# The order of two heads' small products on TensorE: one head after the other, or alternating

## The chip, the cores and the metric

The kernel runs on one core of a Trainium2 chip. The metric is the time of one execution in device microseconds, as the median of several runs.

## What is computed

One layer of a hybrid decoder for 256 prompt tokens and 8 sample tokens (T = 264 columns; activations stand transposed, features on the partitions):

```
x = x + 0.5 * swiglu(rmsnorm(x, n1), f1g, f1u, f1d)
proj = rmsnorm(x, nm) @ w_in                    # 2048 -> 4864
o_att  = sink_attention(q, k, v)                # 16 heads of 64, window 128, blocks of 128
o_rwkv = rwkv_time_mix(proj[..., ATT_COLS:])    # 16 heads of 64, matrix state 64 x 64
x = x + concat(o_att, o_rwkv) @ w_out
x = x + 0.5 * swiglu(rmsnorm(x, n2), f2g, f2u, f2d)
```

The recurrence of one time-mixing head, per token, which the kernel computes for the prompt in four chunks of 64 tokens:

```
sa = S @ (-kk);  S = S * exp(logw) + outer(sa, kk * a) + outer(v, k);  y = S @ r
```

## The kernel before

**The large products.** Both feed-forward parts, the projections (`win`) and the output product (`wout`) go through `gemm`: a chunk of up to 512 weight columns is loaded (`raw`, SP queue), ScalarE casts it to `hi` (line 121), VectorE takes the rest `lo` (line 56), and TensorE does three products per 128 x 128 block with 264 columns. Their results (`acc`) have three banks. Every product goes through the helper `mm`, so most of TensorE's rows carry line 72.

**The mixing stage** (`mixing_body`). The 16 time-mixing heads stand as eight pairs: head 0 of a pair has partitions 0 to 63, head 1 partitions 64 to 127 (`HALF`). The pairs form four batches of two (`BATCH`). Each piece of work is a generator that stops at `yield`; every chunk of a large product calls `tick`, which lets each generator go one step further. The order of calls is `SEQ`: the projections of the four batches, then of keys and values, then of the eight query tiles; then the output product in three passes (`PASS`), ahead of which the tasks that it needs are drained. A scheduler then puts the instructions of each engine in order; each engine works through its own list in that order. Small products (`m`) share five banks (`NM`), taken in turn with `mp()`.

Of the generators, these hold the lines that the change touches:

- `prep` (lines 356 to 458), once per pair: decay and keys, then **Gram blocks** (lines 420 to 433): for each head four products of `BK` (128 columns of one half of the partitions) with `KR` (128 columns) into a bank of the head's own, a masked copy `gm` by VectorE, a transfer of its diagonal blocks to DRAM, and a `yield`. Then two transposes (line 436), the **intermediate keys** `gv` (lines 441 to 446, `gm` with `UV`, 64 x 64 each, both heads in one bank in different partitions), and the transposes of `BK` (lines 447 to 451), which alternate between the heads and use two banks.
- `chain` (lines 470 to 619), once per batch: the diagonal blocks come back (`X`, `Xt`), VectorE solves 30 steps of substitution (`st`, `Xt`), the inverse blocks go out and come back (`TT`). `TN` is their transpose. Then the **corners of the inverse**: 32 x 32 products `gm` with `TN` (lines 515 to 521), copies `zs` (line 525), products `zs` with `TT` (lines 527 to 531), copies into `TT` (line 534). Then **inverse times keys** (`TT` with `KR`, lines 541 to 545) into one bank per pair, copies `W` and `uv`; the **transitions and receptances** (`W` with `BT`, `W` with `gm`, lines 553 to 559), 64 x 64 each, both heads in one bank; products `pN`, `pY`; and three steps over the chunks, whose products with `PT` and `KR` alternate between the heads.
- `attend` (lines 713 to 752), once per query tile, which holds two heads: the two **attention scores** of a head (queries 128 to 255 against 256 keys, queries 0 to 127 against 128 keys, contraction 64) into a bank of its own, the sum with the bias and the maximum (VectorE, line 728), `softmax` (lines 702 to 711), a `yield`; after both heads the transposes of the probabilities (lines 737 to 739) and the products with the values.
- `dec_rwkv` (lines 635 to 667): the state update of the sample tokens, 16 rounds of VectorE and GpSimd work. It and all of batches 0 to 2 are drained ahead of the first pass of the output product, with the attention tasks going on beside them.

In the trace a product stands as out<-moving,weights; a 32-bit product appears as two instructions. `kr,bk` is a Gram block, `uv,gm` with 64 x 64 the intermediate keys, `TN,gm` and `TT,zs` the corners, `kr,TT` inverse times keys, `t,W` and `gm,W` transitions and receptances, `s,q` scores, `C,t` of lines 737 to 739 the transposes of the probabilities.

Of the kernel before, what the change touches and what calls it, by code (L numbers as in the profile page):

```python
# [10 lines left out]
ALU = mybir.AluOpType  # L11
AX = mybir.AxisListType

P = 128
NP = 256
# [9 lines left out]
HALF = (slice(0, 64), slice(64, 128))  # L25
# [20 lines left out]
def body(tc, I, O):  # L46
    nc = tc.nc
    V, A, G, TE, SP = nc.vector, nc.scalar, nc.gpsimd, nc.tensor, nc.sync
# [6 lines left out]
    def tt(e, out, a, b, op):  # L55
        return e.tensor_tensor(out=out, in0=a, in1=b, op=op)  # L56
# [11 lines left out]
    def bc(ap, shape):  # L68
        return ap.broadcast_to(list(shape))

    def mm(out, lhsT, rhs, start=True, stop=True, **k):
        TE.matmul(out, lhsT, rhs, start=start, stop=stop, **k)  # L72
# [20 lines left out]
    with ExitStack() as ctx:  # L93
# [17 lines left out]
        def mp():  # L111
            return pp.tile([P, 512], F32, tag="m", bufs=NM, name=uid("m"))
# [176 lines left out]
        def mixing_body(mx, n2, n3):  # L289
# [12 lines left out]
            tri, msk = C[:, CTR:CTR + P], C[:, CMK:CMK + P]  # L302
# [53 lines left out]
            def prep(p, bt, k, xrr, xk, xv):  # L356
# [39 lines left out]
                BK, KR = ring((P, 4, 3, 64), "bk", 2), ring((P, 3, 4, 64), "kr", NKR)  # L396
# [20 lines left out]
                tt(V, bv, bps[:, :T], xv, ALU.mult)  # L417
                G.tensor_copy(bvdec[:, p, :], bv[:, NP:T])
                yield
                for h in range(2):  # L420
                    r = HALF[h]
                    gp = mp()
                    for c in range(4):
                        mm(gp[:, c * P:(c + 1) * P], BK[r, c, h:h + 2, :], KR[r, 0:2, c, :])
                    gm = ring((P, 4, P), "gm", NGM)
                    bt.Gm[k][h] = gm
                    tt(V, gm, gp.rearrange("p (c t) -> p c t", c=4), bc(msk.unsqueeze(1), (P, 4, P)), ALU.mult)
                    for blk in range(2):
                        x = blk * 32
                        SP.dma_start(  # L430
                            scr[bt.i].rearrange("(h b k c) (s t) -> h b k s c t", h=2, b=2, c=4, s=32)[h, blk, k],
                            gm[h * 64 + x:h * 64 + x + 32, :, x:x + 32])
                    yield
# [5 lines left out]
                        A.copy(KR[HALF[h], 0, e:4:2, :],  # L439
                               kp[HALF[e], :256].rearrange("p (c t) -> p c t", c=2)[:, :, HALF[h]])  # L440
                gv = mp()
                for h in range(2):
                    r, o = HALF[h], HALF[1 - h]
                    for c in range(4):
                        mm(gv[r, c * 64:c * 64 + 64], bt.Gm[k][h][o, c, 0:64], bt.UV[o, c, k, r])
                A.copy(KR[:, 2], gv[:, :256].rearrange("p (c t) -> p c t", c=4))
                bps = [mp(), mp()]
                for c in range(4):
                    for h in range(2):
                        r = HALF[h]  # L450
                        mm(bps[h][:, c * 64:c * 64 + 64], BK[r, c, h:h + 2, :], ident[r, r])
                for tb in range(2):
                    t = tmp((P, 2, P))
# [16 lines left out]
            def chain(bt):  # L470
                n = bt.n
# [17 lines left out]
                for s in range(1, 31):  # L489
                    m, w = -(-s // ng), 31 - s  # L490
                    t = ring((ng * nr, m, w), "st", 2)
# [8 lines left out]
                for h in range(2):  # L500
                    for blk in range(2):
                        x = h * 64 + blk * 32
# [3 lines left out]
                for h in range(2):  # L506
                    for blk in range(2):
                        x = h * 64 + blk * 32
# [4 lines left out]
                    V.transpose(TN[h * 64:h * 64 + 32], TT[h * 64:h * 64 + 32, :, 0:32])  # L513
                yield
                ps = mp()
                for h in range(2):
                    for k in range(n):
                        for c in range(4):
                            j = k * 4 + c
                            mm(ps[h * 64 + 32:h * 64 + 64, j * 32:j * 32 + 32],  # L520
                               bt.Gm[k][h][h * 64:h * 64 + 32, c, 32:64], TN[h * 64:h * 64 + 32, j, :])
                zs = ring((P, n * 4, 32), "zs", 1)
                for h in range(2):
                    r = slice(h * 64 + 32, h * 64 + 64)
                    A.copy(zs[r], ps[r, :n * P].rearrange("p (c t) -> p c t", t=32))
                yield
                ps = mp()
                for h in range(2):
                    r = slice(h * 64 + 32, h * 64 + 64)
                    for j in range(4 * n):  # L530
                        mm(ps[h * 64:h * 64 + 32, j * 32:j * 32 + 32], zs[r, j, :], TT[r, j, 32:64])
                for h in range(2):
                    r = slice(h * 64, h * 64 + 32)
# [5 lines left out]
                N = ring((P, n, 4, 64), "N", 1)  # L539
                wus = [mp() for _ in range(n)]  # L540
                for k in range(n):
                    for h in range(2):
                        r = HALF[h]
                        for c in range(4):
                            mm(wus[k][r, c * P:c * P + P], TT[r, k * 4 + c, :], bt.KR[k][r, 0:3:2, c, :])
                for k in range(n):
                    v = wus[k].rearrange("p (c t) -> p c t", c=4)
# [3 lines left out]
                yield  # L551
                pbs = [mp() for _ in range(n)]
                for k in range(n):
                    for h in range(2):
                        r = HALF[h]
                        for c in range(1, 4):
                            x = (c - 1) * P
                            mm(pbs[k][r, x:x + 64], W[r, k, c - 1, :], bt.BT[k][c // 2][r, c % 2, r])
                            mm(pbs[k][r, x + 64:x + P], W[r, k, c - 1, :], bt.Gm[k][h][r, c, 64:128])
                for k in range(n):  # L560
                    v = pbs[k][:, :384].rearrange("p (c t) -> p c t", c=3)
# [3 lines left out]
                for k in range(n):  # L565
                    for h in range(2):
                        r = HALF[h]
# [3 lines left out]
                for h in range(2):  # L571
                    r = HALF[h]
# [140 lines left out]
            def attend(t, q):  # L713
                p = t // 4
                G.tensor_copy(qd[:, p, :, t % 4], q[:, NP:T])
                bs = [load(I["bias"][(2 * p + h) * 4 + t % 4], (P, 256)) for h in range(2)]
                yield
                sc = []
                for h in range(2):
                    r = HALF[h]  # L720
                    head = (2 * p + h) * 4 + t % 4
                    sps = mp()
                    mm(sps[:, 0:256], q[r, P:NP], kT[p][r, 0:NP])
                    mm(sps[:, 256:384], q[r, 0:P], kT[p][r, 0:P])
                    s1, s0 = tmp((P, 256)), tmp((P, P))
                    mxv = ring((P, 2), "mxv", 6)
                    for s, a, b, j in ((s1, sps[:, 0:256], bs[h], 0), (s0, sps[:, 256:384], bs[h][:, P:256], 1)):
                        V.tensor_tensor_reduce(out=s, in0=a, in1=b, op0=ALU.add, op1=ALU.max, scale=1.0,
                                               scalar=vc(VSK + head), accum_out=mxv[:, j:j + 1])
                    softmax([s1, s0], mxv, vc(VSK + head), 2)  # L730
                    sc.append((s1, s0))
                    yield
                yield from pause(PW[4])
                pt = []
                for s1, s0 in sc:
                    tp = mp()
                    TE.transpose(tp[:, 0:P], s0, ident)  # L737
                    TE.transpose(tp[:, P:2 * P], s1[:, 0:P], ident)
                    TE.transpose(tp[:, 2 * P:3 * P], s1[:, P:256], ident)
                    pa, pb = tmp((P, 256)), tmp((P, P))  # L740
                    A.copy(pa, tp[:, 0:256])
                    V.tensor_copy(pb, tp[:, 256:384])
                    pt.append((pa, pb))
                    yield
                op = mp()
                for h, (pa, pb) in enumerate(pt):
                    r = HALF[h]
                    mm(op[r, 0:256], Vt[p][:, 0, r], pa, True, False)
                    mm(op[r, P:256], Vt[p][:, 1, r], pb, False, True)
                o = slot()  # L750
                A.copy(o[:, :NP], op[:, :NP])
                mixed[8 + t] = o
# [266 lines left out]
```

## Time and profile before

| | |
|---|---|
| Median of 3 runs | 2114.09 us (2106.59 to 2114.15) |
| Profiled execution, its own time | 2113.38 us |
| Span from first to last instruction | 2111.5 us |
| Mean granted TensorE clock | 0.971 |
| Large products into `acc`, instructions | 14736 |
| Transfers | 356.29 MB, mean 169 GB/s |

The profile is that of one execution. Engines are PE (TensorE products), PEld (its weight loads), DVE (VectorE), ACT (ScalarE), POOL (GpSimd) and SP (the queue that issues most transfers). Products are pipelined: the recorded length of one contains its way through the array, so neighbours overlap, and the distance between two starts is the pace. Busy time of a group is the union of its records. A number in brackets with an arrow is idle time ahead of a group and what ended it. The granted clock is the share of full speed that TensorE had.

### The profile page before, as it was taken

The page shows a single profiled execution, that of the slowest core. Times are in us where ns is not written, and L with a number is a line of the kernel's source. Part 1 is how long each engine was busy: PE and PEld are TensorE (multiplying, and loading weights), DVE is VectorE, ACT ScalarE, POOL GpSimd, SP SyncE. Part 2 cuts the span into 40 slices and gives each one's busy share as a digit, 9 for nine tenths or more (in the row PEclk, how much of TensorE's full clock was granted, in tenths as well). Part 3 has the DMA queues.
Part 4 walks back from the last instruction along what each step waited for, and adds up shares of the span by engine and source line. Part 5 has one row for each costly group of instructions (what it writes and reads, how often), then busy time and mean ns, then how long its engine had stood idle before and what let it go on. Part 6 is the DMA issues. An engine that isn't in the chain of part 4 may idle for free.

```text
span 2111.5 us, 45349 instructions
## 1 busy us (share of the span) xinstructions
PE 2045.6 (97%) x16966; PEld 1997.4 (95%) x16966; DVE 1327.7 (63%) x2631; ACT 1061.5 (50%) x2078; POOL 311.1 (15%) x404
## 2 busy tenths in 40 slices
PE   8999999999999999999986899999999999999997
PEld 8999999999999999999975589899999999999997
DVE  5765555556555577876888646756555565655555
ACT  5644444444444576756532444644444444444445
POOL 0301011020101122201044110210110101011012
PEclk9999999999999999999996679999999999999998
DMA  6555565656555574544442155556555565555554
GB/s 221 176 175 187 175 206 170 211 181 181 182 177 185 178 233 150 150 118 129 122 139 79 38 147 183 165 181 181 181 178 184 177 185 182 178 184 175 187 177 139
DMA packets 227535, 356.29 MB, mean 169 GB/s; under 512 B 42177, under 2 KB 83153, under 8 KB 227281
## 3 DMA queue, kind: packets, MB, share of 16 engines
q1 hardware_dynamic: 221616, 344.72, 52.4%
q10 hardware_dynamic: 5696, 8.66, 1.1%
q8 instruction: 133, 2.18, 0.4%
q14 instruction: 90, 0.73, 0.1%
HBM read 345.15 MB, written 10.21 MB: 168 GB/s over the span
## 4 chain that ended last, share of the span: by engine, by line
PE 92%; DVE 4%; DMA 1%; ACT 1%; issue 1%; SPq 0%; DVEq 0%; ACTq 0%
PE acc L72 83%; PE m L72 9%; DVE lo L56 1%; DMA sb<-Xt 0%; DVE ld L56 0%; DMA raw<-in_gu 0%; DVE t L56 0%; DVE st L56 0%; ACT L66 0%; DVE y L56 0%; DVE t L631 0%; DVE s L59 0%; ACT t L66 0%; PE m L737 0%; DVE Xt L56 0%
## 5 line engine op out<-in xcount | busy, mean ns | idle before, releaser
L72 PE MATMUL acc<-s,hi 128*128 128x264 f32 x7072 | 1315.1, 286 | 13.3 <-ACT hi L121 7.7
L56 DVE TENSOR_TENSOR lo<-raw,hi 128x512 fp32r<-128x512 f32 (+2 forms) x1304 | 876.6, 676 | 606.4 <-ACT hi L121 583.2
L121 ACT CAST hi<-raw 128x512 fp32r<-128x512 f32 (+2 forms) x1304 | 780.4, 602 | 879.8 <-PE acc L72 802.2
L72 PEld LDWEIGHTS acc<-s,hi 128*128 128x128 f32 x7072 | 1107.0, 190 | 21.4 <-ACT hi L121 7.7
L72 PE MATMUL acc<-s,lo 128*128 128x264 f32 x3536 | 1013.4, 287 | 2.0 <-DVE lo L56 1.9
L72 PEld LDWEIGHTS acc<-s,lo 128*128 128x128 f32 x3536 | 669.1, 189 | 5.4 <-DVE lo L56 3.9
L72 PE MATMUL acc<-t,hi 128*128 128x264 f32 x2752 | 503.0, 285 | 1.6 <-ACT t L250 1.6
L72 PEld LDWEIGHTS acc<-t,hi 128*128 128x128 f32 x2752 | 426.5, 189 | 1.9 <-ACT t L250 1.8
L72 PE MATMUL acc<-t,lo 128*128 128x264 f32 x1376 | 388.8, 285 | 0.0
L56 POOL TENSOR_TENSOR t<-t,t 128x264 f32<-128x264 f32 (+1 forms) x146 | 156.8, 1074 | 1197.3 <-ACT hi L121 897.5
L72 PEld LDWEIGHTS acc<-t,lo 128*128 128x128 f32 x1376 | 258.4, 188 | 0.0
L56 DVE TENSOR_TENSOR t<-acc,t 128x264 f32<-128x264 f32 x164 | 70.9, 432 | 36.9 <-PE acc L72 36.5
L56 POOL TENSOR_TENSOR s<-s,s 128x264 f32<-128x264 f32 (+1 forms) x56 | 48.7, 871 | 199.0 <-ACT s L66 180.3
L66 ACT ACT_TABLE_LOAD x42 | 53.9, 1283 | 2.9 <-PEq L1011 1.2
L59 DVE SCALAR_TENSOR_TENSOR s<-acc,s 128x264 f32<-128x264 f32 x96 | 40.6, 427 | 16.6 <-PE acc L72 16.1
L59 DVE SCALAR_TENSOR_TENSOR x<-acc,x 128x264 f32<-128x264 f32 x96 | 40.6, 427 | 10.0 <-PE acc L72 9.5
L66 ACT ACTIVATE t<-t 128x264 f32<-128x264 f32 x94 | 40.0, 425 | 3.4 <-DVE t L56 1.9
L250 ACT CAST t<-t 128x264 fp32r<-128x264 f32 x86 | 35.5, 412 | 3.6 <-POOL t L56 2.1
L56 DVE TENSOR_TENSOR st<-X,Xt 128x60 f32<-128x60 f32 (+10 forms) x120 | 28.1, 234 | 12.9 <-DMA Xt<-sa 6.6
L342 POOL COPY shc<-pj 128x9 f32<-128x9 f32 x26 | 20.0, 768 | 85.9 <-DVE pj L56 85.9
L72 PE MATMUL m<-s,hi 128*128 128x264 f32 x160 | 30.3, 289 | 0.3 <-ACT hi L121 0.3
L66 ACT ACTIVATE t<-t,sta 128x256 f32<-128x256 f32 (+2 forms) x33 | 14.7, 446 | 28.3 <-DVE sta L63 27.1
(210 smaller groups left out, 1095.9 us busy)
## 6 DMA issues: line engine op xcount, KB each, us to landing
raw<-in_gu SPq DMA_DIRECT2D x688, 256.0 KB, 3.2
raw<-in_dn SPq DMA_DIRECT2D x224, 256.0 KB, 2.7
raw<-in_win SPq DMA_DIRECT2D x152, 256.0 KB, 3.3
raw<-in_dn SPq DMA_DIRECT2D x160, 192.0 KB, 2.7
raw<-in_wout SPq DMA_DIRECT2D x48, 256.0 KB, 3.0
raw<-in_wout SPq DMA_DIRECT2D x32, 128.0 KB, 2.4
xsp<-x ACTq DMA_DIRECT2D x16, 132.0 KB, 3.5
s<-xsp SPq DMA_DIRECT2D x16, 132.0 KB, 3.0
```

The source lines that it names most:

```text
L56: return e.tensor_tensor(out=out, in0=a, in1=b, op=op)
L59: return V.scalar_tensor_tensor(out=out, in0=a, scalar=s, in1=b, op0=op0, op1=op1)
L66: return A.activation(out=out, in_=in_, func=f, **k)
L72: TE.matmul(out, lhsT, rhs, start=start, stop=stop, **k)
L121: A.copy(hi[:, :w], raw[:, :w])
L250: A.copy(hi, u)
L342: G.tensor_copy(shc[:, t, :], pj[:, NP:NP + NB + 1])
```

## The change

The loops over the two heads of a pair move inside. Gram blocks: both heads take their banks first, and for each chunk head 0's product stands ahead of head 1's; the masked copies, transfers and `yield`s follow per head. Intermediate keys, both corner products, inverse times keys: the loop over heads becomes the innermost. Transitions and receptances: for each chunk both heads' product with `BT`, then both heads' product with `gm`. Scores: both heads take their banks, first the two products with 256 keys, then the two with 128; the softmax follows per head with its `yield`. No product, copy or transfer is added or taken away.

```diff
--- before.py
+++ after.py
@@ -417,14 +417,15 @@
                 tt(V, bv, bps[:, :T], xv, ALU.mult)
                 G.tensor_copy(bvdec[:, p, :], bv[:, NP:T])
                 yield
-                for h in range(2):
-                    r = HALF[h]
-                    gp = mp()
-                    for c in range(4):
-                        mm(gp[:, c * P:(c + 1) * P], BK[r, c, h:h + 2, :], KR[r, 0:2, c, :])
+                gps = [mp(), mp()]
+                for c in range(4):
+                    for h in range(2):
+                        r = HALF[h]
+                        mm(gps[h][:, c * P:(c + 1) * P], BK[r, c, h:h + 2, :], KR[r, 0:2, c, :])
+                for h in range(2):
                     gm = ring((P, 4, P), "gm", NGM)
                     bt.Gm[k][h] = gm
-                    tt(V, gm, gp.rearrange("p (c t) -> p c t", c=4), bc(msk.unsqueeze(1), (P, 4, P)), ALU.mult)
+                    tt(V, gm, gps[h].rearrange("p (c t) -> p c t", c=4), bc(msk.unsqueeze(1), (P, 4, P)), ALU.mult)
                     for blk in range(2):
                         x = blk * 32
                         SP.dma_start(
@@ -439,9 +440,9 @@
                         A.copy(KR[HALF[h], 0, e:4:2, :],
                                kp[HALF[e], :256].rearrange("p (c t) -> p c t", c=2)[:, :, HALF[h]])
                 gv = mp()
-                for h in range(2):
-                    r, o = HALF[h], HALF[1 - h]
-                    for c in range(4):
+                for c in range(4):
+                    for h in range(2):
+                        r, o = HALF[h], HALF[1 - h]
                         mm(gv[r, c * 64:c * 64 + 64], bt.Gm[k][h][o, c, 0:64], bt.UV[o, c, k, r])
                 A.copy(KR[:, 2], gv[:, :256].rearrange("p (c t) -> p c t", c=4))
                 bps = [mp(), mp()]
@@ -513,9 +514,9 @@
                     V.transpose(TN[h * 64:h * 64 + 32], TT[h * 64:h * 64 + 32, :, 0:32])
                 yield
                 ps = mp()
-                for h in range(2):
-                    for k in range(n):
-                        for c in range(4):
+                for k in range(n):
+                    for c in range(4):
+                        for h in range(2):
                             j = k * 4 + c
                             mm(ps[h * 64 + 32:h * 64 + 64, j * 32:j * 32 + 32],
                                bt.Gm[k][h][h * 64:h * 64 + 32, c, 32:64], TN[h * 64:h * 64 + 32, j, :])
@@ -525,9 +526,9 @@
                     A.copy(zs[r], ps[r, :n * P].rearrange("p (c t) -> p c t", t=32))
                 yield
                 ps = mp()
-                for h in range(2):
-                    r = slice(h * 64 + 32, h * 64 + 64)
-                    for j in range(4 * n):
+                for j in range(4 * n):
+                    for h in range(2):
+                        r = slice(h * 64 + 32, h * 64 + 64)
                         mm(ps[h * 64:h * 64 + 32, j * 32:j * 32 + 32], zs[r, j, :], TT[r, j, 32:64])
                 for h in range(2):
                     r = slice(h * 64, h * 64 + 32)
@@ -539,9 +540,9 @@
                 N = ring((P, n, 4, 64), "N", 1)
                 wus = [mp() for _ in range(n)]
                 for k in range(n):
-                    for h in range(2):
-                        r = HALF[h]
-                        for c in range(4):
+                    for c in range(4):
+                        for h in range(2):
+                            r = HALF[h]
                             mm(wus[k][r, c * P:c * P + P], TT[r, k * 4 + c, :], bt.KR[k][r, 0:3:2, c, :])
                 for k in range(n):
                     v = wus[k].rearrange("p (c t) -> p c t", c=4)
@@ -551,11 +552,13 @@
                 yield
                 pbs = [mp() for _ in range(n)]
                 for k in range(n):
-                    for h in range(2):
-                        r = HALF[h]
-                        for c in range(1, 4):
-                            x = (c - 1) * P
+                    for c in range(1, 4):
+                        x = (c - 1) * P
+                        for h in range(2):
+                            r = HALF[h]
                             mm(pbs[k][r, x:x + 64], W[r, k, c - 1, :], bt.BT[k][c // 2][r, c % 2, r])
+                        for h in range(2):
+                            r = HALF[h]
                             mm(pbs[k][r, x + 64:x + P], W[r, k, c - 1, :], bt.Gm[k][h][r, c, 64:128])
                 for k in range(n):
                     v = pbs[k][:, :384].rearrange("p (c t) -> p c t", c=3)
@@ -716,12 +719,15 @@
                 bs = [load(I["bias"][(2 * p + h) * 4 + t % 4], (P, 256)) for h in range(2)]
                 yield
                 sc = []
+                spp = [mp(), mp()]
                 for h in range(2):
                     r = HALF[h]
+                    mm(spp[h][:, 0:256], q[r, P:NP], kT[p][r, 0:NP])
+                for h in range(2):
+                    r = HALF[h]
+                    mm(spp[h][:, 256:384], q[r, 0:P], kT[p][r, 0:P])
+                for h, sps in enumerate(spp):
                     head = (2 * p + h) * 4 + t % 4
-                    sps = mp()
-                    mm(sps[:, 0:256], q[r, P:NP], kT[p][r, 0:NP])
-                    mm(sps[:, 256:384], q[r, 0:P], kT[p][r, 0:P])
                     s1, s0 = tmp((P, 256)), tmp((P, P))
                     mxv = ring((P, 2), "mxv", 6)
                     for s, a, b, j in ((s1, sps[:, 0:256], bs[h], 0), (s0, sps[:, 256:384], bs[h][:, P:256], 1)):
```

## The prediction

> **What bounds the kernel now.** I read the page's busy shares, its clock row and its chain first, and then cut the mixing stage into stretches. In the page the reader is to see that TensorE is nearly always busy and carries the chain, and that the clock row dips in one place only.
>
> ```profile
> span 2111.5 us, 45349 instructions
> ...
> PE 2045.6 (97%) x16966; PEld 1997.4 (95%) x16966; DVE 1327.7 (63%) x2631; ACT 1061.5 (50%) x2078; POOL 311.1 (15%) x404
> ...
> PEclk9999999999999999999996679999999999999998
> ...
> PE 92%; DVE 4%; DMA 1%; ACT 1%; issue 1%; SPq 0%; DVEq 0%; ACTq 0%
> ```
>
> All edited products lie between 800 and 1231 us, so I cut that part where the waits change. Columns of the windows view: stretch, length, busy time of PE, PEld, DVE, ACT, POOL, granted clock, DMA share, GB/s.
>
> ```profile
> 800.00:1066.00 266.00, 264.37 (x2518) 248.65 (x2518) 201.25 (x519) 170.88 (x397) 44.27 (x93) 0.99 0.48 133
> 1066.00:1138.00 72.00, 53.77 (x466) 48.39 (x464) 70.67 (x203) 23.92 (x59) 36.24 (x46) 0.85 0.39 115
> 1138.00:1145.50 7.50, 0.00 (x0) 0.00 (x0) 1.40 (x5) 0.00 (x0) 0.00 (x0) 0.50 0.52 121
> 1145.50:1178.50 33.00, 32.00 (x297) 26.86 (x298) 20.48 (x62) 7.98 (x28) 9.79 (x14) 0.61 0.11 33
> 1178.50:1198.00 19.50, 10.64 (x32) 6.87 (x29) 13.52 (x44) 10.62 (x23) 4.16 (x8) 0.67 0.18 51
> 1198.00:1230.80 32.80, 30.91 (x111) 19.63 (x110) 19.60 (x82) 15.87 (x59) 4.39 (x13) 0.50 0.31 92
> 1230.80:1262.00 31.20, 30.90 (x284) 28.86 (x284) 13.63 (x36) 11.75 (x26) 0.00 (x0) 0.91 0.53 154
> ```
>
> I call them A, B, W, C, D, E and F. **A** (preparation of the pairs, batches 0 to 2) is TensorE's: 264.37 of 266 us, full clock. **B** is VectorE's (70.67 of 72): the last batch's substitution and the sample's state update. W is transfers. **C** (corners to states of the last batch) and **E** (the last attention heads) are TensorE's again, at 0.61 and 0.50 of the clock. D between them is waits, F the first output products. A microsecond of TensorE time saved in A, C or E is worth up to one; in B, W, D about nothing.
>
> **The change part by part.** It removes and adds no product: it changes the order in which the two heads' products stand, head by head before, alternating now. Head 0's operands lie in partitions 0 to 63 and head 1's in 64 to 127, so neighbours now use different rows of the array. Does TensorE run such neighbours side by side? The kernel has alternating groups already. The first fence has one pair's Gram blocks (kr,bk, by head), its keys (uv,gm, by head) and its BK transposes (C,bk, alternating, two banks); the second the chain's first products (N,PT and kr,N, alternating); the third one batch's inverse times keys (kr,TT, by head). Columns: start, length, group; the next row's start ends a group.
>
> ```profile
> 818.25 1.71 PE L72 MATMUL m<-kr,bk 64*128 64x128 f32 x16
> 819.88 0.33 PE L436 MATMUL m<-C,kr 128*128 128x128 f32 x1
> ...
> 822.45 0.96 PE L72 MATMUL m<-uv,gm 64*64 64x64 f32 x16
> 823.34 1.11 PE L72 MATMUL m<-C,bk 64*128 64x64 f32 x16
> 824.38 0.38 PE L72 MATMUL m<-ld,tw 65*128 65x128 f32 x1
> ```
> ```profile
> 1173.45 0.45 PE L72 MATMUL m<-N,PT 64*64 64x64 f32 x8
> 1173.73 0.40 PE L72 MATMUL m<-kr,N 64*64 64x64 f32 x8
> 1174.06 0.33 PE L737 MATMUL m<-C,t 128*128 128x128 f32 x1
> ```
> ```profile
> 918.91 2.56 PE L72 MATMUL m<-kr,TT 64*64 64x128 f32 x32
> 921.40 0.39 PE L72 MATMUL acc<-s,lo 128*128 128x264 f32 x1
> ```
>
> Yes. Sixteen alternating 128-column loads take 823.34 to 824.38 = 1.04 us, where sixteen by head take 819.88 - 818.25 = 1.63. Sixteen alternating 64-column instructions take 1174.06 - 1173.45 = 0.61, where sixteen by head (uv,gm) take 0.89. N,PT writes both heads into one bank and is as fast as that.
>
> [...]
>
> Now the sum for A, which holds eight preparations, three batches' corners and two batches' keys and transitions. In this view: instructions, then busy us, mean ns.
>
> ```profile
> L72 PE MATMUL m<-t,W 64*64 64x64 f32 x48 | 4.7, 227 | 0.0
> L72 PE MATMUL m<-gm,W 64*64 64x64 f32 x48 | 4.6, 219 | 0.0
> L72 PE MATMUL m<-TN,gm 32*32 32x32 f32 x96 | 4.2, 207 | 1.0 <-DVE TN L513 1.0
> L72 PE MATMUL m<-TT,zs 32*32 32x32 f32 x96 | 3.3, 193 | 0.0
> ```
>
> - Gram blocks: 1.63 to 1.04, 0.59 x 8 = 4.7. The moving side is 128 columns where C,bk has 64, which bounds the gain between 0 and 4.7; I take 4.7, since kr,TT, also 128 columns, does 32 in 2.49 us, when at the Gram rate it would be 3.3: its heads already overlap where they meet.
> - gv, the intermediate keys: 0.89 to 0.61, 0.28 x 8 = 2.2.
> - inverse times keys (kr,TT): 1.04 and 8 more pairs at the by-head pace of one instruction, 1.63 / 16 = 0.10, 1.86 for 2.49, 0.6 x 2 = 1.2.
> - transitions and receptances (t,W with gm,W, interleaved, so about 4.8 us together, 2.4 a batch): 24 pairs, of which 8 in 0.61 and 16 at 0.89 / 16 = 0.056, 1.5 us; 0.9 x 2 = 1.8.
> - corners: 7.5 us in six groups; no alternating 32-column group is shown, so between 0 and half, 3.7; the ends of a group don't shrink, I take 0.35 x 6 = 2.1.
>
> A: 12.0 us. New waits in A: the keys now need both heads' masked Gram blocks from the first instruction on.
>
> ```profile
> L56 DVE TENSOR_TENSOR gm<-m,C x16: 678/684/692, 819.4 to 1055.3; 128x512 f32<-128x512 f32 x16
> ```
>
> The second block is 0.68 us later. Before the keys the built order still has the key transposes and some 20 projection products, which took 2.6 us before (819.88 to 822.45), and they hide it; without that cover it would cost at most 0.7 x 8 = 5.5 us. The same holds for the corners, whose first product now stands alone ahead of projections in batch 0, with the rest behind.
>
> **B**: two pairs of scores and one batch's keys and transitions get shorter, but VectorE ends this stretch with the same work as before, so 0 (bound: 0.8 x 2 + 0.6 + 0.9 + 0.4 = 3.5).
>
> **C**, rows of that stretch alone:
>
> ```profile
> L72 PE MATMUL m<-kr,TT 64*64 64x128 f32 x32 | 7.3, 421 | 0.4 <-ACT TT L534 0.4
> L72 PE MATMUL m<-t,W 64*64 64x64 f32 x24 | 4.0, 320 | 0.0
> ...
> L72 PE MATMUL m<-s,q 64*128 64x256 f32 x8 | 3.8, 570 | 0.0
> ...
> L72 PE MATMUL m<-TT,zs 32*32 32x32 f32 x32 | 2.1, 237 | 0.5 <-ACT zs L525 0.5
> L72 PE MATMUL m<-TN,gm 32*32 32x32 f32 x32 | 2.1, 236 | 10.8 <-DVE TN L513 10.8
> ...
> L72 PE MATMUL m<-s,q 64*128 64x128 f32 x8 | 2.0, 344 | 0.0
> ```
>
> Here kr,TT has no overlap at all (7.3 us, where twice 2.49 is 5.0): the scheduler had put both pairs' head 0 first and head 1 later. Alternating: 7.3 to 3.7 (16 pairs at twice 0.10, and the ends), saving 3.6; transitions 4.0 to 2.9 (24 pairs at half clock, 0.11 each, and the ends), 1.1; corners 4.2 to 2.4, 1.8; two pairs of scores 5.8 to 3.3, 2.5. Together 9.0. Against it: before, head 0's half of the chain ran ahead and head 1's filled TensorE during the copies; now both heads stand at each copy together. The built order leaves nothing between first and second corner, so two zs copies and their hand-over show; from the 0.4 and 0.5 us idle above, three such places cost about 1.5. C: 7.5 (bounds 3 and 9).
>
> **D**: one pair of scores, in a stretch of waits: 1.0 (bounds 0 and 1.6).
>
> **E**, six heads of scores, and the transposes' wait:
>
> ```profile
> L72 PE MATMUL m<-s,q 64*128 64x256 f32 x12 | 7.3, 711 | 0.0
> L72 PE MATMUL m<-s,q 64*128 64x128 f32 x12 | 3.8, 417 | 0.0
> L737 PE MATMUL m<-C,t 128*128 128x128 f32 x8 | 3.7, 465 | 1.9 <-DVE t L63 1.9
> ```
>
> 11.1 us become 11.1 / 2 plus the ends, 6.4: 4.7 saved. What is late next is the softmax on VectorE: its wait of 1.9 grows to about 3.1, so E gives 3.5 (bounds 1.5 and 4.7). The scores of a pair now hold two of the five small banks at once; nothing in E shows a wait for a bank, and I price it at 0 inside these bounds.
>
> Sum: 12.0 + 7.5 + 1.0 + 3.5 = 24.0 us. The profiled execution took 2113.38 us (2111.5 of span and 1.9 around), 0.7 under the median 2114.09: 2113.38 - 24.0 = **2089.4 us**.
>
> **The rivals.**
>
> [...]
> - *A's gain is absorbed.* VectorE is busy 201.25 of 266 us in A and does the splits that feed TensorE; if its chain sets B's start, A's 12.0 go: 2101.4. Against it: TensorE idles 1.6 us in A. 0.15.
> [...]
> - *Lock step.* In C to E each copy and softmax stands bare, and the tail loses 8 us instead of gaining 12: 2113.38 - 12.0 + 8 = 2109.4. 0.05.
> [...]
>
> **How the numbers follow.** Forecast 0.56. A measurement of this kernel can tell about 0.5%, 10.6 us, so the line is 2103.5. Faster: 0.56 + 0.12, and of the two rivals near 2101.5, whose own spread crosses the line, 0.13 of 0.21: 0.81. Same: the other 0.08 and lock step: 0.13. Slower: 0.06. The forecast with the bounds of C, E and the corners runs from 2083 to 2097; the range takes in the opening clock below and the two rivals above: 2077 to 2103; outside are lock step, the slower case and the edges, about 0.2.
>
> **What would show it.** In the profile after: Gram groups of 16 in about 1.04 us, keys in 0.61, kr,TT of 32 in 1.9 in A and 3.7 in C, scores of a pair in the time of one head. 800 to 1066 shrinks by 12 us, B stays at 72, C is near 25, E near 29. Wrong would be: same-bank groups at the old pace; A shorter and B longer by as much; idle before TT,zs or C,t grown by more than 3 us; the clock row longer low.

## The result and the profile after

The changed kernel takes 2098.69 us in the median of 8 runs (2095.97 to 2106.43); the kernel before, run on the same chip, takes 2113.19 us in the median of 8 (2106.59 to 2114.16). The ratio is 0.9944, 95% interval 0.9928 to 0.9961: 0.56% faster, with the interval from 0.39% to 0.72%. In time, 11.8 us by the ratio and 14.5 us by the two medians. The forecast was 24.0 us less (2089.4). The measured time lies in the range (2077 to 2103), but only about half of the forecast saving came. Medians count every execution; the ratios, here and below, leave out one slow one (5005 us, of the kernel with the scores only).

The profiled execution took 2099.58 us, 13.8 us less than the one of before. Its page has the lines that answer to those shown of before:

```profile
span 2097.8 us, 45345 instructions
...
PE 2012.9 (96%) x16966; PEld 1967.4 (94%) x16966; DVE 1323.0 (63%) x2631; ACT 1060.3 (51%) x2078; POOL 310.2 (15%) x404
...
PEclk9999999999999999999996789999999999999998
...
PE 88%; DVE 7%; DMA 3%; ACT 1%; issue 1%; SPq 1%; DVEq 0%; ACTq 0%
```

TensorE is busy 32.7 us less, yet the span is only 13.7 us shorter, and in the chain of work that ended last TensorE's share fell from 92% to 88% while VectorE's rose from 4% to 7% and the transfers' from 1% to 3%. Saved TensorE time has become waiting for others. Where, the windows tell; the stretches A, B, W, C, D, E, F are cut at about the same places as before; A begins at 800 us both times and ends 0.5 us ahead of the last substitution in the kernel before, 2.3 us ahead of it in the kernel after (columns: stretch, length, busy time of PE, PEld, DVE, ACT, POOL, granted clock, DMA share, GB/s).

```profile
800.00:1064.00 264.00, 260.54 (x2571) 243.54 (x2570) 203.41 (x525) 172.72 (x402) 45.68 (x97) 0.99 0.49 138
1064.00:1136.00 72.00, 46.66 (x424) 41.01 (x422) 68.30 (x199) 21.77 (x55) 32.67 (x43) 0.80 0.37 110
1136.00:1142.60 6.60, 0.00 (x0) 0.00 (x0) 1.25 (x3) 0.00 (x0) 0.00 (x0) 0.50 0.32 64
1142.60:1168.00 25.40, 22.08 (x300) 17.89 (x300) 21.47 (x72) 7.98 (x28) 10.38 (x15) 0.75 0.13 43
1168.00:1184.00 16.00, 7.97 (x28) 4.61 (x30) 11.76 (x36) 9.33 (x22) 4.11 (x6) 0.75 0.22 62
1184.00:1217.00 33.00, 23.43 (x114) 15.39 (x115) 17.98 (x81) 18.23 (x61) 4.29 (x13) 0.71 0.32 91
1217.00:1248.00 31.00, 30.63 (x279) 28.65 (x277) 13.45 (x35) 10.56 (x25) 0.00 (x0) 0.89 0.54 155
```

C is 7.6 us shorter, D 3.5, E not at all. A is 2 us shorter. In B the length is 72 us as before, but TensorE's idle time in it rose from 72 - 53.77 = 18.2 to 72 - 46.66 = 25.3 us: here most of what A saved lies idle. From the start of the last substitution to the first corner, it idled 25.8 of 79.1 us before and 32.1 of 76.5 after.

A window's edge is a choice, so the same is read from events. The rows are of the tiles `s` (the first sums of squares for the norm that opens the mixing stage), `st` (the last batch's substitution), `TN` (its first corners) and `qd` (the first product after the prompt's attention); each gives durations and then first to last start. First before, then after:

```profile
L72 PE MATMUL m<-s,ones x4: 385/386/387, 774.0 to 774.7; 128*128 128x264 f32 x4
L56 DVE TENSOR_TENSOR st<-X,Xt x30: 163/219/722, 1066.5 to 1135.1; 128x60 f32<-128x60 f32 x4, 128x28 f32<-128x28 f32 x2, 128x48 f32<-128x48 f32 x2, 128x42 f32<-128x42 f32 x2
L72 PE MATMUL m<-TN,gm x32: 228/236/256, 1145.6 to 1149.8; 32*32 32x32 f32 x32
L72 PE MATMUL m<-qd,ld x64: 248/250/373, 1228.0 to 1245.3; 64*128 64x4 f32 x64
```
```profile
L72 PE MATMUL m<-s,ones x4: 385/386/386, 775.3 to 775.9; 128*128 128x264 f32 x4
L56 DVE TENSOR_TENSOR st<-X,Xt x30: 155/210/742, 1066.3 to 1135.0; 128x60 f32<-128x60 f32 x4, 128x28 f32<-128x28 f32 x2, 128x48 f32<-128x48 f32 x2, 128x42 f32<-128x42 f32 x2
L72 PE MATMUL m<-TN,gm x32: 228/236/255, 1142.8 to 1146.2; 32*32 32x32 f32 x32
L72 PE MATMUL m<-qd,ld x64: 249/249/373, 1214.2 to 1230.2; 64*128 64x4 f32 x64
```

| From | to | before | after | less | forecast |
|---|---|---|---|---|---|
| start of mixing | last substitution begins (A) | 292.5 | 291.0 | 1.5 | 12.0 |
| last substitution begins | first corner (B, W) | 79.1 | 76.5 | 2.6 | 0 |
| first corner | first `qd` product (C, D, E) | 82.4 | 71.4 | 11.0 | 12.0 |
| together | | 454.0 | 438.9 | 15.1 | 24.0 |

(The stage begins 1.3 us later in the trace of after, which is why the two executions are 13.8 us apart and not 15.1.) The half behind the corners came out nearly as forecast in its sum, the half ahead of them did not.

**Was TensorE's time in A saved at all?** The groups of A, after, in the view by line and shape (busy us, mean ns):

```profile
L72 PE MATMUL acc<-s,hi 128*128 128x264 f32 x932 | 181.5, 291 | 0.0
L72 PE MATMUL acc<-s,lo 128*128 128x264 f32 x466 | 134.7, 291 | 1.7 <-DVE lo L56 1.4
L72 PE MATMUL m<-kr,bk 64*128 64x128 f32 x128 | 9.3, 285 | 0.0
L72 PE MATMUL m<-uv,gm 64*64 64x64 f32 x128 | 7.4, 226 | 0.0
L72 PE MATMUL m<-kr,TT 64*64 64x128 f32 x64 | 3.9, 272 | 0.0
L72 PE MATMUL m<-t,W 64*64 64x64 f32 x48 | 3.0, 222 | 0.0
L72 PE MATMUL m<-gm,W 64*64 64x64 f32 x48 | 2.9, 218 | 0.0
L72 PE MATMUL m<-TT,zs 32*32 32x32 f32 x96 | 2.3, 193 | 0.0
L72 PE MATMUL m<-TN,gm 32*32 32x32 f32 x96 | 2.3, 192 | 0.6 <-DVE TN L514 0.6
```
And those of before in its A, as far as they are not shown yet:
```profile
L72 PE MATMUL acc<-s,hi 128*128 128x264 f32 x897 | 176.4, 293 | 0.0
L72 PE MATMUL acc<-s,lo 128*128 128x264 f32 x448 | 129.8, 292 | 0.7 <-DVE lo L56 0.5
L72 PE MATMUL m<-kr,bk 64*128 64x128 f32 x128 | 13.7, 285 | 0.0
L72 PE MATMUL m<-uv,gm 64*64 64x64 f32 x128 | 8.1, 224 | 0.0
L72 PE MATMUL m<-kr,TT 64*64 64x128 f32 x64 | 5.1, 276 | 0.0
```

Yes: the seven small groups fell from 13.7 + 8.1 + 5.1 + 4.7 + 4.6 + 4.2 + 3.3 = 43.7 us to 31.1. `t,W` and `gm,W` lie over each other; counted once, the two together fell from 4.9 to 3.2, and the seven by 10.9. The transposes of `BK` (`C,bk`), which now stand among the keys, took 0.9 us more (11.5 to 12.4), so about 10.0 us of TensorE's time were saved.

Where they went shows between events (from the start of mixing to the start of the last substitution, and from there to the first corner; the two windows above do not begin at the same point of the work). Ahead of the substitution stand 1595 projection instructions instead of 1556, behind it 184 instead of 225: some 40 changed places. Neighbours of that kind, recorded at 291 ns each, start 0.12 us apart in the timeline of after, so the 39 took 4.7 us. The third batch's `kr,TT` (1.9 us) also begins ahead of the substitution now, at 1064.3 us; before it began at 1067.8. TensorE's idle time there grew by 1.8 us (1.63 to 3.46), and 1.5 us came out: together the 10. The scheduler had put later work into the time that the small products left free.

### The profile page after: what moved, and what is told of

The parts are those of the page before. It is cut to its first block, busy times and chain, and to the rows that moved or that the text cites. A ratio compares the mean times of both kernels' runs of the same rounds, so it can differ in the third digit from the quotient of the medians.

```text
span 2097.8 us, 45345 instructions
## 1 busy us (share of the span) xinstructions
PE 2012.9 (96%) x16966; PEld 1967.4 (94%) x16966; DVE 1323.0 (63%) x2631; ACT 1060.3 (51%) x2078; POOL 310.2 (15%) x404
## 4 chain that ended last, share of the span: by engine, by line
PE 88%; DVE 7%; DMA 3%; ACT 1%; issue 1%; SPq 1%; DVEq 0%; ACTq 0%
PE acc L72 82%; PE m L72 6%; DVE lo L56 1%; DMA raw<-in_gu 1%; DVE ld L56 1%; ACT t L66 0%; DMA TT<-sb 0%; DVE t L56 0%; DVE Xt L56 0%; DVE t L63 0%; DVE st L56 0%; DVE t L734 0%; ACT L66 0%; DVE s L59 0%; DMA sb<-Xt 0%
## 5 line engine op out<-in xcount | busy, mean ns | idle before, releaser
L56 DVE TENSOR_TENSOR st<-X,Xt 128x60 f32<-128x60 f32 (+10 forms) x120 | 25.9, 216 | 18.1 <-DMA Xt<-sa 11.8
L404 POOL COPY XD<-t 128x8 f32<-128x8 f32 x40 | 18.4, 461 | 86.0 <-DVE t L59 80.1
L56 DVE TENSOR_TENSOR Xt<-Xt,st 128x60 f32<-128x60 f32 (+10 forms) x120 | 27.1, 226 | 1.7
```

Source lines behind the costliest of these rows:

```text
L404: G.tensor_copy(XD[:, i, p, :], src[:, NP:T])
```

## The experiments

Two theories. **T**, the forecast's: A is bound by TensorE, and what is saved there comes out. **P**, its rival: A's saving is absorbed, since the last batch's preparation, transfers and substitution have a pace that TensorE does not set. Each ratio below is to the kernel before in the same series of runs; "us" worked out from a ratio is that share of 2113.

### Parts of the change alone

The kernel before with Gram blocks and intermediate keys of the change only:

```diff
+                gps = [mp(), mp()]
+                for c in range(4):
+                    for h in range(2):
+                        r = HALF[h]
+                        mm(gps[h][:, c * P:(c + 1) * P], BK[r, c, h:h + 2, :], KR[r, 0:2, c, :])
...
+                for c in range(4):
+                    for h in range(2):
+                        r, o = HALF[h], HALF[1 - h]
                         mm(gv[r, c * 64:c * 64 + 64], bt.Gm[k][h][o, c, 0:64], bt.UV[o, c, k, r])
```

> The kernel before, with only the Gram blocks and the intermediate keys alternating. Theory P (pulled forward): the TensorE time saved in the preparations is real, some 6 us, but it is filled with projection products that the order draws forward and that are missing later, in a stretch that VectorE ends; the time is within 3 us of before, -3 to 0. Rival T (TensorE sets the pace up to 1066 us, as the prediction had it): -6.9 us (4.7 + 2.2).

Measured: 2110.58 us, ratio 0.9984 (0.9969 to 0.9999), 3.4 us less. T had 6.9; the interval reaches to 6.6, so it leaves T out, but narrowly.

With corners, inverse times keys, transitions and receptances only (the edits at `chain`):

> The kernel before, with only the corners, inverse times keys, transitions and receptances alternating. Theory P: only the last batch's part counts, which lies behind the substitution: -7 to -10 us. Rival T: 5.1 us ahead of 1066 us and 6.5 behind, less 1.5 of lost cover: -10 us, of which the first half shows as an earlier start of the last substitution (by 5 us); under P that start moves by less than 2 us.

Measured: 2106.25 us, ratio 0.9969 (0.9957 to 0.9981), 6.6 us less (4.0 to 9.1), where P had 7 to 10 and T 10. The last substitution began at 1067.6 us, counted from the start of mixing 0.5 us earlier than before, where T had 5: what the first batches saved in A did not arrive there, and the gain is that of the last batch's chain.

With the scores only (the edit at `attend`):

> The kernel before, with only the scores alternating. Prediction's terms: -7 us (2.5 + 1.0 + 3.5). Theory L (the last heads are bound by softmax on VectorE and ScalarE once TensorE is faster, since TensorE idles 9.6 of 33 us there in the changed kernel): -2 to -4 us.

Measured: 2105.46 us, ratio 0.9963 (0.9949 to 0.9976), 7.8 us less. That is what the forecast had for the scores (2.5 + 1.0 + 3.5 = 7.0); the expectation that the softmax would hide half of it was wrong. The three parts alone add up to 17.8 us where the whole change has 11.8; the intervals are too wide to tell whether the parts hinder each other.

The other way round, the kernel after with Gram blocks and keys by head again, as before:

> The changed kernel with the Gram blocks and the intermediate keys by head again. Theory P: the preparations' part is worth 0 to 3 us, so 2098.7 to 2102 us. Rival T (TensorE sets the pace up to 1066 us): 6.9 us above the changed kernel, 2105.6 us. Sum of the two parts measured alone: 7.4 + 8.2 = 15.6 us under the kernel before.

Measured: 2100.65 us, ratio 0.9945 (0.9931 to 0.9959), where the kernel after has 0.9944 (0.9928 to 0.9961). The Gram part, over half of A's term (6.9 of 12.0), is worth 0 to 2 us beside the other two. Even from the low end of one interval to the high end of the other it is 6.6 us, less than T's 6.9: T falls, though not by much.

In the traces the stage itself does move. Counted from the start of mixing, the last substitution begins at 294.3 us here and at 291.0 in the kernel after, and the first corner comes at 372.4 and 367.5; 3.1 us of this come back behind the corner, where 68.3 us pass to the first `qd` product instead of 71.4. In the kernel before, alternating Gram blocks and keys alone made the substitution begin later (295.1 for 292.5) and the first corner come at 370.7 for 371.6. So little of the Gram part is left in the total, but single traces do not agree on the place at which it is lost.

### The same work twice

If A were TensorE's, adding to it must cost as much as saving gains. The kernel after, with each Gram block computed twice into the same bank:

```diff
-                for c in range(4):
+                for c in [0, 1, 2, 3] * 2:
```

> The changed kernel, with each Gram product computed twice into the same bank: about 0.9 us more on TensorE per pair, 7.2 us in all, ahead of 1066 us. Nothing else is added. Theory P: under 3 us above the changed kernel (2098.7 us), since TensorE has slack before the last substitution ends. Rival T: 7 to 9 us above it.

Measured: 2101.77 us, ratio 0.9943 (0.9926 to 0.9959), 0 to 3 us more than after; T had 7 to 9, and the ends of the two intervals lie 6.6 us apart. In the stretch from 800 to 1066 of this kernel:

```profile
L72 PE MATMUL m<-kr,bk 64*128 64x128 f32 x256 | 16.4, 278 | 0.0
L72 PE MATMUL m<-uv,gm 64*64 64x64 f32 x128 | 7.9, 238 | 4.6 <-DVE gm L56 4.6
```

The Gram groups take 7.1 us more of TensorE than after (16.4 against 9.3), and the total hardly moves. Projections made room: ahead of the last substitution stand 1523 of their instructions instead of 1595, between it and the first corner 256 instead of 184, and TensorE's idle time in that second part falls from 32.1 to 26.1 us. In the kernel after TensorE is busy 260.54 of A's 264 us, and still its time there is worth little in the total: the share is filled up with products that can as well be done later, while TensorE idles in B. In this trace too the stage moves: the substitution begins 4.2 us later than after, counted from the start of mixing, and the first corner comes 7.6 us later; 2.8 us of it come back behind the corner.

### What sets the end of B

First suspect: VectorE, whose update of the sample tokens' state lies in B with the substitution. Both kernels without that update:

```diff
+                S = load(I["st"][:, 0:n, :], shp)
                 for k in range(64 // n):
                     r = slice(k * n, k * n + n)
-                    S = load(I["st"][:, r, :], shp)
...
+                    SP.dma_start(O["wkvs"][:, r, :], S)
+                    tt(G, yr[:, r], XR[:, 0, r], XR[:, 5, r], ALU.mult)
                     yield
...
-                    tt(G, t2, S, bj(5), ALU.mult)
-                    V.tensor_reduce(out=yr[:, r], in_=t2, op=ALU.add, axis=AX.X)
```

> The kernel before without the sample tokens' state update (the 16 rounds of VectorE and GpSimd work are left out, one tile is loaded and stored 16 times; new_wkv_sample and y_sample are not computed). Some 20 us of VectorE work leave the stretch from 1066 to 1138 us. If VectorE ends that stretch: 15 to 25 us below the kernel before. It is the base for the next run.

> The changed kernel without the same state update. Theory P (in the preparations TensorE's saving only draws projection products forward, and they find VectorE in their way): with VectorE's load gone the products drawn forward (24 to 30 instructions, 3 to 4 us, and the shorter groups behind them) count, so the distance to the run without the change grows from 14.5 us to 17 to 21 us. Rival: the preparations' saving is lost for good, and the distance stays at 14.5 us or falls, since the tail is less loaded.

Measured: before without the update 2072.35 us (ratio 0.9805, 0.9787 to 0.9823), after without it 2059.46 us (0.9749, 0.9733 to 0.9765). The update weighs 41 us, far more than expected: the substitution then takes 26 us instead of 69. (The edit also takes away GpSimd's share of the update and 15 of the 16 loads, so not all of the 41 us need be VectorE's.) But the distance between the two orders is 12.9 us, no larger than the 11.8 to 14.5 with the update; the expectation of 17 to 21 was a miss. With VectorE free, A's saving still does not come out: counted from the start of mixing, the first corner comes at 342.0 us instead of 343.4. The waits of VectorE between 1055 and 1080 us, after without the update, show what took over:

```profile
DVE st L56 <- DMA Xt<-sa: 10.3, 1, 10.3
```

The last substitution begins at 1072.8 us there, when its transfer has landed; VectorE sits ready for 10.3 us. So behind VectorE stands a second limit, the last pair's Gram block and the transfers of its diagonal blocks. Counted from the start of mixing, the last masked block stands at 282.7 us here and at 282.6 in the kernel before without the update: the shorter groups did not move it.

The same wait in the kernel after, and before it was changed (VectorE's waits from 1056 to 1070):

```profile
DVE st L56 <- DMA Xt<-sa: 5.5, 1, 5.5
```
```profile
DVE st L56 <- DMA Xt<-sa: 2.7, 1, 2.7
```

The last masked Gram block began 2.4 us earlier (1052.9 for 1055.3), 3.7 counted from the start of mixing, and the wait for `Xt` grew by 2.8. The start of the substitution stayed. The earlier block did reach the queue, which issued its last `Xt` at 1061.9 us instead of 1064.4; but from there to the start of the substitution 4.4 us passed instead of 2.1. Why that last transfer was slower is open.

So the transfers were pulled forward alone: after, with the loads of `Xt` issued by ScalarE instead of behind those of `X` on SP:

```diff
-                    SP.dma_start(Y[g * nr:(g + 1) * nr],
+                    A.dma_start(Y[g * nr:(g + 1) * nr],
```

> The changed kernel, with the loads of Xt issued on ScalarE's queue and those of X left on SP's: eight issues of 0.6 us in a row become two rows of four, ahead of each substitution. In the changed kernel VectorE waited 5.5 us for Xt. If this wait sets the start of the last substitution: it begins 2 to 4 us earlier and the time is 2 to 4 us under the changed kernel (2098.7 us). If VectorE's other work sets the end of the stretch: the same time, within 1 us.

Measured: 2099.22 us, ratio 0.9937 (0.9922 to 0.9952): no difference to after. The row of the tile `st`:

```profile
L56 DVE TENSOR_TENSOR st<-X,Xt x30: 171/210/594, 1063.1 to 1136.7; 128x60 f32<-128x60 f32 x4, 128x28 f32<-128x28 f32 x2, 128x48 f32<-128x48 f32 x2, 128x42 f32<-128x42 f32 x2
```

It begins 3.2 us earlier than after and ends 1.7 us later, with 11 rounds of the update beside it as after; VectorE is busy 71.1 of the 73.6 us between. An earlier start alone is absorbed by VectorE's shared list.

Then VectorE was relieved, with one of the update's operations on ScalarE, on top of after, on top of before, and on top of after together with the two queues:

```diff
-                    tt(V, t2, bc(sa[:, r].unsqueeze(2), shp), bj(2), ALU.mult)
+                    for j in range(n):
+                        act(t2[:, j, :], XR[:, 2, :], AF.Copy, scale=sa[:, k * n + j:k * n + j + 1])
```

> The kernel after, with one VectorE operation of each round of the sample state's update moved to ScalarE (the product of sa with XR, one 128x256 instruction becomes four scaled copies of 64 columns). In 1064 to 1136 us of the kernel after, ten such instructions take 5.2 us of VectorE's 68.3. Theory P (VectorE's list sets the end of the last substitution, so that TensorE time saved ahead of it comes out as nothing): the substitution ends 3 to 5 us earlier counted from the mixing start and the time falls by 3 to 5 us against the kernel after. Rival (transfers and the order of the preparations set it, VectorE only waits): 0 to 1.5 us.

> The kernel before with the same move of one VectorE operation a round to ScalarE. Theory P: VectorE was what ended that stretch before the change too, so it gains the same 3 to 5 us against the kernel before, and the distance between the two orders stays near 12 to 14 us. Rival: the gain of the Gram part comes out once VectorE is lighter, and the distance grows to 17 or more.

> The kernel after with that VectorE operation on ScalarE and the loads of X and Xt issued by ScalarE. The second alone let the last substitution begin 3.2 us earlier and moved nothing at its end. Theory P: with a lighter VectorE the earlier start comes out too, 5 to 8 us under the kernel after in all. Rival (VectorE's load decides nothing, or the start does not): no better than the first alone.

| Kernel | median, us | ratio to before | mixing start to first corner | first corner to `qd` |
|---|---|---|---|---|
| before | 2111.89 | 1 | 371.6 | 82.4 |
| before, relieved | 2109.64 | 0.9984 (0.9972 to 0.9995) | 368.4 | 79.7 |
| after | (other series) | 0.9944 (0.9928 to 0.9961) | 367.5 | 71.4 |
| after, two queues | 2099.22 (other series) | 0.9937 (0.9922 to 0.9952) | 370.2 | 68.6 |
| after, relieved | 2093.36 | 0.9911 (0.9897 to 0.9924) | 368.3 | 66.2 |
| after, relieved, two queues | 2088.55 | 0.9895 (0.9880 to 0.9910) | 359.4 | 67.4 |

After, relieved: 7.0 us less than after by the ratios, more than the 3 to 5 that P said, but in another place. The end of the substitution did not move (1134.9 us; it began 2.1 us later, its `Xt` landing later once more); the gain stands behind the corners, where the last four of the sixteen rounds lie. Three kernels with no such relief (two queues, Gram blocks twice, Gram blocks by head) have 68.3 to 68.6 us there, so even this place is not certain. As to B, the expectation was a miss. Before, relieved: 3.4 us less by the ratio, and the distance between the two orders is 15.4 us, between what P (12 to 14) and its rival (17 or more) had said: this one decides nothing.

Both together: 10.4 us less than after by the ratios, and 22.2 us (1.05%) less than before, the fastest version of the study. Here the first corner comes 8.1 us earlier than after, which neither of the two edits gave alone. The substitution's row:

```profile
L56 DVE TENSOR_TENSOR st<-X,Xt x30: 164/222/726, 1063.3 to 1121.0; 128x60 f32<-128x60 f32 x4, 128x28 f32<-128x28 f32 x2, 128x48 f32<-128x48 f32 x2, 128x42 f32<-128x42 f32 x2
```

It ends 14.0 us earlier than after; 5.7 of that is lost again between its end and the first corner (1121.0 to 1134.5 us, where after has 1135.0 to 1142.8). The order of VectorE's list changed with it: 8 rounds of the update lie beside the substitution instead of 11, and the other three stand in the wait for the transfers behind it, where VectorE is now busy 13.3 of 13.5 us and in the kernel after 1.7 of 7.8. From the start of the substitution to the first corner VectorE has 70.2 us of work here and 69.7 in the kernel after. So of the 8.1 us the earlier start gave 2.8, and the rest came from filling VectorE's idle time, not from a shorter list.

In the total, both edits together are 3.4 us better than the relief alone by the ratios, and the intervals of the two overlap. The runs show that VectorE's work weighs on B, that the start of the last substitution hangs on a transfer, and that TensorE's time in A counts for little in the total; that the two limits hide each other is argued from the place of the first corner in one trace each, not shown by the time.

## Why the prediction was wrong

**The step that failed** is the first one: "A is TensorE's: 264.37 of 266 us, full clock ... a microsecond of TensorE time saved in A, C or E is worth up to one", and with it the term A, 12.0 us. Counted to the start of the last substitution it gave 1.5 us, and 4.1 to the first corner. It is the rival "A's gain is absorbed" that came in its outcome, though not by the chain that it named: at B's start VectorE was not late but waited 5.5 us for a transfer. The 0.15 given to it was argued down with TensorE's 1.6 us of idle time in A. That number does not speak against it. A was full because the scheduler draws projection products into it, and the place to look was the next stage, B, where TensorE idled 18.2 of 72 us: what A no longer had to do drew work forward out of B, and TensorE idles there instead. That the time still fell inside the range says little for the sum: the range had been drawn to take in this rival.

Inside A all terms but one were nearly right as TensorE time: 10.0 us of the 12.0. Gram blocks 13.7 to 9.3, 4.4 (forecast 4.7). Inverse times keys 5.1 to 3.9, 1.2 (1.2). Corners 7.5 to 4.6, 2.9 (2.1, the bound was 3.7). Transitions and receptances, counted once, 4.9 to 3.2, 1.7 (1.8). Only the keys gained nothing (2.2 forecast): their rows fell by 0.7, but in the built order the transposes of `BK` now stand among them and took 0.9 more, as TensorE's timeline in the first pair shows.

```profile
823.74 0.33 PE L72 MATMUL m<-uv,gm 64*64 64x64 f32 x2
823.99 0.44 PE L72 MATMUL m<-C,bk 64*128 64x64 f32 x4
824.36 0.68 PE L72 MATMUL m<-uv,gm 64*64 64x64 f32 x14
824.96 0.89 PE L72 MATMUL m<-C,bk 64*128 64x64 f32 x12
825.78 0.71 PE L72 MATMUL m<-ld,tw 65*128 65x128 f32 x4
```

Both groups together take 825.78 - 823.74 = 2.04 us, where before they took 1.93.

**B at 0** was nearly right: the substitution takes 68.7 us as before (68.6); the 2.6 us came between its end and the first corner, for a reason that no run isolates.

**C at 7.5** came out at 7.6, in part by luck. Its rows after:

```profile
L72 PE MATMUL m<-kr,TT 64*64 64x128 f32 x32 | 4.7, 423 | 0.5 <-ACT TT L535 0.5
...
L72 PE MATMUL m<-s,q 64*128 64x256 f32 x8 | 1.9, 570 | 0.0
...
L72 PE MATMUL m<-TT,zs 32*32 32x32 f32 x32 | 1.4, 238 | 0.5 <-ACT zs L526 0.5
L72 PE MATMUL m<-TN,gm 32*32 32x32 f32 x32 | 1.3, 237 | 13.7 <-DVE TN L514 13.7
...
L72 PE MATMUL m<-s,q 64*128 64x128 f32 x8 | 1.0, 344 | 0.0
```

Scores 5.8 to 2.9 (3.3 forecast), corners 4.2 to 2.7 (2.4), inverse times keys 7.3 to 4.7 (3.7); transitions and receptances, counted once, 4.3 to 2.3 (4.0 to 2.9). These last fell further: the granted clock had risen ahead of most of them (0.61 to 0.75 over C), and the median of one was 218 ns where before, at 0.50, it was 312. The sum had not counted this, and it made up for the smaller gain of the inverse times keys. TensorE's idle time in C grew by 2.3 us (1.5 priced). The idle time ahead of `TT,zs` is 0.5 us as before: the lock step did not come.

**D and E at 4.5** gave 3.5 and -0.2, together 3.3. D has more than the 1.0 priced, E less than its 3.5. E's scores fell further than forecast, from 11.1 us to 4.0, also at a higher clock (0.50 to 0.71), but E is 33.0 us long as before (32.8). TensorE's waits in E, after (us in total, times, longest):

```profile
PE acc L72 <- ACT s L865: 3.2, 1, 3.2
PE m L743 <- DVE sta L63: 3.1, 1, 3.1
PE m L743 <- DVE t L63: 2.5, 3, 1.0
PE m L72 <- ACT t L747: 0.6, 1, 0.6
```

Before, the transposes' wait of 1.9 us was the only one. Now TensorE waits 9.4 us in this stretch, for the softmax and for the split of the output product (`s`, line 865). The forecast had let the transposes' wait grow to 3.1; it grew to 5.6, and the split's 3.2, which the forecast did not have, stands behind it.

**The other chances.** In the chances and the range stand three terms that no run shows and that were the author's estimates: 0.12 for a clock that opens in the tail, with the range's 2077; 0.06 for a slower outcome; and 0.06 of the 0.21 for a time near 2101.5 in which only Gram blocks and scores gain (4.7 + 2.5 + 1.0 + 3.5 = 11.7 us). What the runs showed in their place:

- The clock in the tail did rise (C 0.61 to 0.75, E 0.50 to 0.71), but the time did not follow, since E then waited for others.
- The kernel did not get slower.
- The other groups gained too: `kr,TT`, corners and transitions, which share a bank, shrank as the two-bank groups did, and the chain part alone gave 6.6 us. In A, at a clock of 0.99 both times, the 96 second corner instructions (`TT,zs`), both heads into different partitions of one bank, have 2.3 us of busy time where by head they had 3.3.

What stays open: at which place the saving is lost when only one part of the change is made, since single traces differ there by some us; why the last pair's preparation does not move ahead of the drawn-forward projections in the built order, and what the time would be if it did. That was not tried.

## What to carry to other kernels

A stage in which an engine is 98% busy is not bound by it if a scheduler fills it with work that could be done later. Before pricing a saving there, look at the next place where that engine waits and ask what ends that wait: if the saved work's successors idle there already, the saving is worth little, here 1.5 to 4.1 us of 12.0. And where two limits may stand one behind the other, moving one can show nothing, as the earlier transfers did here: try both together before calling either worthless.

## What the runs showed of the hardware

The granted clock was not the same for the two orders. With only the chain's products alternating, its mean was 0.70 from 1143 to 1169 us and 0.72 from 1169 to 1200; with only the scores alternating, it was 0.50 and 0.76. (Columns as in the windows above; the chain kernel first.)

```profile
1143.00:1169.00 26.00, 21.44 (x276) 17.52 (x276) 19.95 (x63) 7.23 (x25) 8.56 (x12) 0.70 0.15 42
1169.00:1200.00 31.00, 21.48 (x98) 13.98 (x96) 23.28 (x84) 17.40 (x52) 5.43 (x9) 0.72 0.17 50
```
```profile
1143.00:1169.00 26.00, 21.53 (x201) 18.96 (x202) 16.52 (x46) 6.19 (x21) 8.74 (x12) 0.50 0.14 41
1169.00:1200.00 31.00, 22.98 (x168) 15.36 (x166) 25.46 (x89) 14.51 (x49) 5.60 (x9) 0.76 0.16 50
```

TensorE is busy 21.44 and 21.53 us in the first of these stretches, nearly equal, at very different clocks. So stretches of nearly equal recorded busy time had different clocks here.

The means hide a step. In windows of 4 us the kernel before has 0.50 from 1140 to 1168 us, 0.56 in the next window and 1.00 from 1172 to 1180; the kernel after has 0.50 from 1140 to 1152, 0.57 in the next and 1.00 from 1156 to 1172. So the clock rises in both, about 26 us behind the first corner before and about 13 us behind it after. In the second stretch of the two fences the means are nearly the same (0.72 and 0.76), though the scores stand in different orders. What decides the moment of the rise, no run shows. E before, with TensorE busy 30.91 of 32.80 us, stayed at 0.50.
